# The order of high and low matrix products in a decoder trunk, and the rows that they read

## The chip, the core and the metric

The kernel runs on one core of a Trainium2 chip. The metric is the time of one execution on the device in microseconds; three runs of the kernel before were taken, and their median counts. Beside the runs there is a profile, which records one execution instruction by instruction.

A core has engines that work side by side: TensorE (PE) for matrix products, with a queue of weight loads that overlaps them (PEld), VectorE (DVE), ScalarE (ACT), GpSimd (POOL), and SyncE (SP), which here issues transfers. On-chip memory (SBUF) has 128 partitions; the products collect in banks of a second memory (PSUM) of 2048 bytes per partition each.

## What is computed

One step of a decoder trunk of one layer, for 256 prompt tokens and 8 x 4 sample tokens, 288 columns in all:

```python
def trunk_layer(x, hist_conv, hist_pool, pos0, ...):
    h = rmsnorm(x, norm1_g)
    proj = jnp.einsum("btd,de->bte", h, w_in) + b_in
    a, gate, z = proj[..., :D_CONV], proj[..., D_CONV:2 * D_CONV], proj[..., 2 * D_CONV:]
    u = a * jax.nn.sigmoid(gate)
    u_ext = jnp.concatenate([hist_conv.astype(u.dtype), u], axis=1)
    c = jax.nn.silu(layernorm(depthwise_causal_conv(u_ext, conv_w, conv_b), ln_g, ln_b))
    z_ext = jnp.concatenate([hist_pool.astype(z.dtype), z], axis=1)
    d = multiscale_pool(z_ext, pos0)
    p = jnp.einsum("btgc,gce->btge", d, pool_w).reshape(bsz, T, D_POOL) * pool_scale
    mix = jnp.concatenate([c, p], axis=-1)
    x = x + jnp.einsum("btm,md->btd", mix, w_out)
    h2 = rmsnorm(x, norm2_g)
    f = jnp.square(jax.nn.relu(jnp.einsum("btd,df->btf", h2, w_ff1)))
    x = x + jnp.einsum("btf,fd->btd", f, w_ff2)
    return x, u_ext[:, -(CONV_W - 1):], z_ext[:, -(POOL_MAX - 1):]
```

The model width is 2048, the hidden width of the MLP 8192, and all data are float32. After the layer comes one more RMSNorm.

## The kernel before

**Layout.** Channels lie on the partitions, the 288 tokens along the free dimension. A block is 128 channels: 2048 channels are 16 blocks. The weights come from memory in tiles of 1024 rows by 256 columns, two loads of 512 KB each, in an order that the host has laid out.

**High and low parts.** The products run in a rounded float32 format (`F32R`). To keep precision, every operand is split into a high part, its rounded value, and a low part, what the rounding left over. For the weights ScalarE casts a loaded tile `wr` into `whi` (line 257), and VectorE (262), GpSimd (265) or a transfer that adds (260) makes `wlo`. Each of these pools holds five tiles of four blocks of rows by 256 columns. The activations are split by ScalarE and VectorE in the same way, into tiles called `hx`, `dx`, `mx`, `ax` and `fx` by stage.

**The rows of an activation tile.** `act2` (line 117) makes a tile for two neighbouring channel blocks m = 0 and 1. It has four rows of 288 float32 numbers, 1152 bytes each, in the order low 0, high 0, low 1, high 1. So row 0 of a partition starts at byte 0, row 1 at 1152, row 2 at 2304, row 3 at 3456. Two of the `ax` pairs use a stretch of an older tile (`ax45`, line 565) in the same order, and the last two pairs use tiles of two rows each, low then high (line 570).

**The matrix routine.** `gemm` (line 283) takes a list of PSUM banks and a list `rhs` of channel blocks as (high, low) pairs. For every block k, and within it for every bank m, it issues three products with a weight tile of 128 x 128 as the stationary operand and a row of 288 columns as the moving operand: high weights x high row (297), high weights x low row (298), low weights x high row (299). The dropped fourth, low x low, is below the precision wanted. All of a bank's products add up in that bank. Usually there are two banks, one for each 128 columns of the weight tile; the first call has four.

**The stages**, in the order of time: the first call on `hx` for two channel blocks of the convolution at once, while the first weights arrive; then the rest of w_in on `hx`, with the depthwise convolution on VectorE and GpSimd (line 415), the gates and the pooling between; the four small pool products on `dx` (`pool_products`); w_out on `dx` and `mx`; then four rounds of eight calls with w_ff1 on `ax`, whose results become `fx`, and eight calls with w_ff2 on `fx`. A call with 16 blocks and two banks has 96 products, and there are 8112 products in all. The first call has 192, w_ff1 and w_ff2 have 3072 each.

**What sets the order.** The order of the engine queues is made when the kernel is built, by a scheduler with a simulated timeline: it takes the lines in program order and moves instructions forward that it believes ready. `between` and `issue_after` hold a few of them in place. In the first call the scheduler shuffles the products of the four banks; in the other calls they stay in program order. The ring of five tiles in each weight pool decides when ScalarE may cast the next tile: after the last product that reads the old one.

Of the kernel before, what the change touches and what calls it, by code (L numbers as in the profile page):

```python
# [10 lines left out]
F32R = mybir.dt.float32r  # L11
# [5 lines left out]
P = 128  # L17
# [3 lines left out]
T = SEQ + NB * NS  # L21
# [62 lines left out]
def trunk_kernel(ctx: ExitStack, tc: tile.TileContext, io):  # L84
# [3 lines left out]
    nc = tc.nc  # L88
# [5 lines left out]
    actp = ctx.enter_context(tc.tile_pool(name="actp", bufs=8))  # L94
# [8 lines left out]
    def nm(s):  # L103
        seen[s] = seen.get(s, 0) + 1
        return f"{s}{seen[s]}"
# [8 lines left out]
    def row(name):  # L114
        return rowp.tile([P, T], F32, name=nm(name), tag="row")

    def act2(name, **kw):

        t = actp.tile([P, 2, 2, T], F32R, name=nm(name), **(kw or {"tag": "act"}))
        return t[:, :, 1, :], t[:, :, 0, :]  # L120

    def tmp(name, n=T, tag="tmp", bufs=2):
        return tmpp.tile([P, n], F32, name=nm(name), tag=tag, bufs=bufs)
# [4 lines left out]
    def f32(t):  # L128
        return t.bitcast(F32)
# [15 lines left out]
    def v(key, j):  # L145
        return vec[:, OFF[key] + j : OFF[key] + j + 1]
# [136 lines left out]
    def gemm(banks, rhs, m_outer=False, between={}):  # L283


        n = len(rhs)
        gets = ready.pop()
        order = [(k, m) for k in range(n) for m in range(len(banks))]
        if m_outer:
            order.sort(key=lambda km: km[1])  # L290
        for k, m in order:
            if m == 0:
                ahead = between[k]() if k in between else None
            (xh, xl), b = rhs[k], banks[m][:, :T]
            wh, wl = gets[k // 8](k % 8, m)
            with tc.issue_after(ahead.ins) if ahead is not None else nullcontext():
                nc.tensor.matmul(b, wh, xh, start=k == 0, stop=False)  # L297
                nc.tensor.matmul(b, wh, xl, start=False, stop=False)  # L298
                last = nc.tensor.matmul(b, wl, xh, start=False, stop=k == n - 1)  # L299
        ready.extend(itertools.islice(weights, 1))  # L300
        return last.ins

    def bank2():
        return acc.tile([P, 2, 512], F32, name=nm("ac"), tag="ac")

    def each(bk):
        return [bk[:, m, :] for m in range(2)]

    def halves(x2):

        return [(x2[0][:, m, :], x2[1][:, m, :]) for m in range(2)]
# [4 lines left out]
    def first_split(k0, n):  # L316
        for k in range(k0, k0 + n):
            if k % 2 == 0:
                hx.extend(halves(act2("hx")))
            hh, hl = hx[k]  # L320
            nc.scalar.activation(hh, xT[:, k, :], AF.Copy, scale=v("norm1_g", k))
            nc.vector.scalar_tensor_tensor(out=hl, in0=xT[:, k, :], scalar=v("norm1_g", k), in1=f32(hh), op0=ALU.mult, op1=ALU.subtract)
        if k0 % 2 == 0:
            firsts.append([by_pair(t) for t in spl()])
        at = slice(k0 % 2, k0 % 2 + n)
        raw, hi, lo = (t[:, :, at, :] for t in (raws[k0 // 2], *firsts[k0 // 2]))
        split_part(raw, None, hi, lo, "V")
# [58 lines left out]
    def conv_products(i, **kw):  # L386
        history(i)
        banks = each(bank2())
        gemm(banks, hx, **kw)
        return banks  # L390
# [38 lines left out]
    def pool_group(g):  # L429
        nc.sync.dma_start(z_all[:, 2 * g : 2 * g + 2, ZO:ZL], io["hist_p"][:, 2 * g : 2 * g + 2, :])  # L430
        bk = bank2()
        gemm(each(bk), hx)
        z = z_all[:, 2 * g : 2 * g + 2, :]
        tz = tmpp.tile([P, 2, T], F32, name=nm("tz"), tag="ag", bufs=2)
        nc.vector.tensor_tensor(tz, bk[:, :, :T], both(rb), op=ALU.mult)
        for m in range(2):
            b_in = v("b_in", 16 + 2 * g + m)
            nc.scalar.activation(z[:, m, PH:ZO], tz[:, m, 0:SEQ], AF.Identity, bias=b_in)
            nc.scalar.activation(samples(z[:, m, ZO:ZL], ZS)[:, :, PH:ZS], samples(tz[:, m, SEQ:T], NS), AF.Identity, bias=b_in)
        s, w = z, 1  # L440
        while w < WINDOWS[g]:
            s2 = tmpp.tile([P, 2, ZL], F32, name=nm("s"), tag="s", bufs=2)
            for m in range(2):
                nc.gpsimd.tensor_tensor(s2[:, m, 2 * w - 1 :], s[:, m, 2 * w - 1 :], s[:, m, w - 1 : ZL - w], op=ALU.add)
            s, w = s2, 2 * w
        d = tmpp.tile([P, 2, T], F32, name=nm("d"), tag="ag2", bufs=2)
        first_sums = s[:, :, PH : PH + w - 1]
        nc.gpsimd.tensor_tensor(first_sums, first_sums, rcnt[:, None, w - 2 : 2 * w - 3].to_broadcast([P, 2, w - 1]), op=ALU.mult)
        nc.vector.scalar_tensor_tensor(out=d[:, :, 0:SEQ], in0=s[:, :, PH:ZO], scalar=1.0 / w, in1=z[:, :, PH:ZO], op0=ALU.mult, op1=ALU.subtract)  # L449
        news = [x[:, :, ZO:ZL].rearrange("p m (b t) -> p m b t", t=ZS)[:, :, :, PH:] for x in (s, z)]  # L450
        for m in range(2):
            nc.gpsimd.tensor_scalar(news[0][:, m], news[0][:, m], 1.0 / w, None, op0=ALU.mult)
            nc.gpsimd.tensor_tensor(samples(d[:, m, SEQ:T], NS), news[0][:, m], news[1][:, m], op=ALU.subtract)
        dh, dl = act2("dx", tag="p", bufs=4)
        nc.scalar.copy(dh, d)
        nc.vector.tensor_tensor(dl, d, f32(dh), op=ALU.subtract)  # L456
        dd[g] = dh, dl
# [3 lines left out]
    def pool_products(g):  # L461

        bk = ms("pp")
        gemm(each(bk), halves(dd[g]))
        for m, (mh, ml) in enumerate(halves(dd[g])):
            i = 2 * g + m
            nc.scalar.activation(mh, bk[:, m, :T], AF.Copy, scale=v("pool_scale", i))
            nc.vector.scalar_tensor_tensor(out=ml, in0=bk[:, m, :T], scalar=v("pool_scale", i), in1=f32(mh), op0=ALU.mult, op1=ALU.subtract)
            mixp[i] = (mh, ml)
# [62 lines left out]
    for g in range(8):  # L532
        bk = bank2()
        with behind:
            last = gemm(each(bk), [mixp[k] for k in korder], between=BETWEEN.get(g, {}))
# [5 lines left out]
    for j, c in enumerate(cs):  # L541
        n = tmpp.tile([P, 2, T], F32, name=nm("n"), tag="ag", bufs=2)
        nc.vector.tensor_tensor(n, c, norm["rows"][:, None, :].to_broadcast([P, 2, T]), op=ALU.mult)
        for m in range(2):
            i = 2 * j + m
            nc.scalar.activation(n[:, m, :], n[:, m, :], AF.Silu, bias=v("ln_b", i), scale=v("ln_g", i))
        mh, ml = act2("mx")
        nc.scalar.copy(mh, n)
        nc.vector.tensor_tensor(ml, n, f32(mh), op=ALU.subtract)
        mixc += halves((mh, ml))  # L550
# [4 lines left out]
    for g in range(8):  # L555
        bk = bank2()
        gemm(each(bk), mixc)
        x2 = xT[:, 2 * g : 2 * g + 2, :]
        nc.vector.tensor_tensor(x2, x2, bk[:, :, :T], op=ALU.add)
        if g < 4:  # L560
            a2 = halves(act2("ax", tag="p", bufs=4))
        elif g < 6:
            if g == 4:
                ax45 = zp.tile([P, N8 * ZL], F32R, name="ax45", tag="z")
                ax45 = ax45[:, 32 : 32 + 8 * T].rearrange("p (g m q t) -> p g m q t", g=2, m=2, q=2)
            a2 = halves((ax45[:, g - 4, :, 1, :], ax45[:, g - 4, :, 0, :]))
        else:
            a2 = []
            for m in range(2):
                t2 = actp.tile([P, 2, T], F32R, name=nm("ax"), tag="c", bufs=4)  # L570
                a2.append((t2[:, 1, :], t2[:, 0, :]))
        for m, (ah, al) in enumerate(a2):
            k = 2 * g + m
            xk = xT[:, k, :]
            nc.scalar.activation(ah, xk, AF.Copy, scale=v("norm2_g", k))
            nc.vector.scalar_tensor_tensor(out=al, in0=xk, scalar=v("norm2_g", k), in1=f32(ah), op0=ALU.mult, op1=ALU.subtract)
            x1.append((ah, al))
            if k == 0:
                nc.scalar.activation(ss2, xk, AF.Square)
            else:  # L580
                q2 = tmp("q")
                nc.scalar.activation(q2, xk, AF.Square)
                nc.gpsimd.tensor_tensor(ss2, ss2, q2, op=ALU.add)
# [4 lines left out]
    for ch in range(DFF // FCH):  # L588
        fx = []
        for g in range(FCH // 256):  # L590
# [4 lines left out]
            t = tmpp.tile([P, 2, T], F32, name=nm("t"), tag="ag", bufs=2)  # L595
# [7 lines left out]
        last = ch == DFF // FCH - 1  # L603
        for g in range(8):
            bk = bank2()
            banks = each(bk)
# [3 lines left out]
            for m in range(2):  # L610
                k = 2 * g + m
# [79 lines left out]
```

## Time and profile before

| | |
|---|---|
| runs, device time | 1106.66, 1105.6, 1106.64 us; median 1106.64 |
| profiled execution, first to last instruction | 1103.1 us |
| outside that span, against the three runs | 2.5 to 3.6 us |
| granted TensorE clock, mean over the span | 0.996 |
| memory traffic | 185.68 MB read, 4.28 MB written |

The profile's page has no time for its own execution apart from the span; the runs lie 2.5 to 3.6 us above that.

How to read the lines that follow. An instruction is named by its line in the kernel and by what it writes and reads, as in `ac<-ax,whi`: the bank `ac` from activations `ax` and high weights `whi`. `x1024` is a count. In the groups, the first number after the bar is the busy time in us and the second the mean of one in ns; then comes the idle time of the engine just before, with what ended it. Products are pipelined: one lasts longer in the records than the distance to the next, so that their rate is read from the starts. In the view by stretches each row has the window, its length, then busy time and count of PE, PEld, DVE, ACT and POOL, the granted clock, the busy share of the DMA engines and GB/s; where the view is for one engine, only that engine stands there.

### The profile page before, as it was taken

How to read it: one execution, taken by the hardware profiler on the slowest of the kernel's cores; microseconds unless marked ns; L12 is line 12 of the kernel's file. 1: busy time of each engine (PE TensorE's matmuls, PEld its weight loads, DVE VectorE, ACT ScalarE, POOL GpSimd, SP SyncE). 2: the span in 40 equal slices, each digit the busy share in tenths (PEclk: the TensorE clock that was granted, in tenths of full speed). 3: DMA queues.
4: the chain of work that ended last, by engine and by line, in shares of the span. 5: the costliest groups of instructions: out<-in, count | busy, mean ns of one | idle time of the engine just before them, and what ended most of it. 6: DMA issues, size and time to landing. Idle time of an engine off the chain costs nothing.

```text
span 1103.1 us, 19716 instructions
## 1 busy us (share of the span) xinstructions
PE 1087.3 (99%) x8204; PEld 1085.0 (98%) x8204; DVE 638.2 (58%) x814; ACT 477.8 (43%) x585; POOL 179.1 (16%) x209
## 2 busy tenths in 40 slices
PE   9999999999999999999999999999999999999996
PEld 8999999999999999999999999999999999999996
DVE  7889999787555444445544444545544445554553
ACT  8654445565544433333443333444433334444441
POOL 0879989512000000000000000000000000000000
PEclk9999999999999999999999999999999999999998
DMA  9996568555555555555555555555555555555522
GB/s 334 279 275 176 155 159 245 168 169 162 166 161 170 168 162 168 171 161 165 170 167 162 171 163 165 171 168 161 169 170 160 168 171 164 165 170 163 164 75 86
DMA packets 58265, 191.24 MB, mean 173 GB/s; under 512 B 6208, under 2 KB 11328, under 8 KB 58176
## 3 DMA queue, kind: packets, MB, share of 16 engines
q1 hardware_dynamic: 56752, 185.53, 53.7%
q0 software_dynamic: 1152, 4.19, 2.1%
q8 instruction: 64, 1.05, 0.4%
q10 hardware_dynamic: 272, 0.26, 0.1%
q14 instruction: 25, 0.20, 0.0%
HBM read 185.68 MB, written 4.28 MB: 172 GB/s over the span
## 4 chain that ended last, share of the span: by engine, by line
PE 89%; DVE 8%; DMA 1%; issue 1%; ACT 1%; POOL 0%; SPq 0%; DVEq 0%; POOLq 0%
PE ac L297 30%; PE ac L299 30%; PE ac L298 29%; DVE pc L415 3%; DVE wlo L262 1%; DMA wlo<-in_w 1%; DVE xT L631 0%; DMA wr<-in_w 0%; DVE c L421 0%; POOL prd L419 0%; DVE q L521 0%; DVE dx L456 0%; DVE c L515 0%; PE pt L242 0%; DVE d L449 0%
## 5 line engine op out<-in xcount | busy, mean ns | idle before, releaser
L257 ACT CAST whi<-wr 128x1024 fp32r<-128x1024 f32 (+1 forms) x341 | 355.6, 1043 | 570.8 <-PE ac L298 537.1
L262 DVE TENSOR_TENSOR wlo<-wr,whi 128x1024 fp32r<-128x1024 f32 (+1 forms) x295 | 363.1, 1231 | 353.4 <-ACT whi L257 352.3
L297 PE MATMUL ac<-ax,whi 128*128 128x288 f32 x1024 | 303.2, 296 | 0.0
L297 PE MATMUL ac<-fx,whi 128*128 128x288 f32 x1024 | 303.1, 296 | 0.0
L299 PE MATMUL ac<-ax,wlo 128*128 128x288 f32 x1024 | 301.9, 295 | 0.0
L299 PE MATMUL ac<-fx,wlo 128*128 128x288 f32 x1024 | 301.9, 295 | 0.0
L298 PE MATMUL ac<-ax,whi 128*128 128x288 f32 x1024 | 298.5, 292 | 0.0
L298 PE MATMUL ac<-fx,whi 128*128 128x288 f32 x1024 | 298.5, 292 | 0.0
L298 PEld LDWEIGHTS ac<-fx,whi 128*128 128x128 f32 x1024 | 192.5, 188 | 0.0
L298 PEld LDWEIGHTS ac<-ax,whi 128*128 128x128 f32 x1024 | 192.5, 188 | 0.0
L297 PEld LDWEIGHTS ac<-ax,whi 128*128 128x128 f32 x1024 | 192.4, 188 | 0.0
L297 PEld LDWEIGHTS ac<-fx,whi 128*128 128x128 f32 x1024 | 192.4, 188 | 0.0
L299 PEld LDWEIGHTS ac<-ax,wlo 128*128 128x128 f32 x1024 | 191.5, 187 | 0.0
L299 PEld LDWEIGHTS ac<-fx,wlo 128*128 128x128 f32 x1024 | 191.5, 187 | 0.0
L297 PE MATMUL ac<-hx,whi 128*128 128x288 f32 x384 | 113.4, 298 | 1.3 <-ACT whi L257 1.3
L299 PE MATMUL ac<-hx,wlo 128*128 128x288 f32 x384 | 110.9, 295 | 1.0 <-DMA wlo<-in_w 0.8
L298 PE MATMUL ac<-hx,whi 128*128 128x288 f32 x384 | 111.4, 292 | 0.0
L265 POOL TENSOR_TENSOR wlo<-wr,whi 128x512 fp32r<-128x512 f32 x76 | 103.8, 1413 | 37.0 <-ACT whi L257 35.5
L415 DVE SCALAR_TENSOR_TENSOR pc<-u_all,vec,pc 128x256 f32<-128x256 f32 x232 | 99.7, 481 | 3.5 <-ACT pc L412 2.3
L297 PEld LDWEIGHTS ac<-hx,whi 128*128 128x128 f32 x384 | 72.3, 189 | 1.7 <-ACT whi L257 1.7
L299 PEld LDWEIGHTS ac<-hx,wlo 128*128 128x128 f32 x384 | 71.2, 188 | 1.5 <-DMA wlo<-in_w 1.0
L298 PEld LDWEIGHTS ac<-hx,whi 128*128 128x128 f32 x384 | 72.2, 188 | 0.0
(117 smaller groups left out, 826.8 us busy)
## 6 DMA issues: line engine op xcount, KB each, us to landing
wr<-in_w SPq DMA_DIRECT2D x335, 512.0 KB, 3.8
wlo<-in_w POOLq DMA_DIRECT2D x8, 512.0 KB, 7.3
xT<-in_xT SPq DMA_DIRECT2D x7, 288.0 KB, 8.0
wr<-in_w SPq DMA_DIRECT2D x5, 256.0 KB, 3.7
out_u_out<-u_all SPq DMA_DIRECT2D x1, 1208.0 KB, 8.6
out_yT<-xT SPq DMA_DIRECT2D x2, 576.0 KB, 2.9
u_all<-in_hist_c SPq DMA_DIRECT2D x8, 136.0 KB, 5.4
out_z_out<-z_all SPq DMA_DIRECT2D x1, 668.0 KB, 9.1
```

Of the source, the lines that this page charges most:

```text
L257: nc.scalar.copy(hi, raw)
L262: nc.vector.tensor_tensor(lo, raw, f32(hi), op=ALU.subtract)
L265: nc.gpsimd.tensor_tensor(lo[:, j : j + 2, :], raw[:, j : j + 2, :], f32(hi[:, j : j + 2, :]), op=ALU.subtract)
L297: nc.tensor.matmul(b, wh, xh, start=k == 0, stop=False)
L298: nc.tensor.matmul(b, wh, xl, start=False, stop=False)
L299: last = nc.tensor.matmul(b, wl, xh, start=False, stop=k == n - 1)
L415: nc.vector.scalar_tensor_tensor(out=dst, in0=up[:, w : w + SEQ], scalar=cwv[:, w : w + 1], in1=pc, op0=ALU.mult, op1=ALU.add)
```

## The change

A call of `gemm` with two banks now takes the blocks in pairs. For a pair and a bank it issues six products: high x high for the first block and the second, low weights x high row for the first and the second, then high weights x low row for the second and the first. So the high rows are read four times in a row and the low rows twice. The call with four banks keeps one block at a time and its order of three.

The rows of an activation tile are now low 0, high 0, high 1, low 1. The six products read rows 1, 2, 1, 2, 3, 0, which start at bytes 1152, 2304, 1152, 2304, 3456 and 0. The tiles with two rows (the last two `ax` pairs) hold low, high for m = 0 and high, low for m = 1. Nothing else changes: the number of products, their operands and the sums are the same. The products of a call add up in another order.

```diff
+    def rows(t):
+
+        return t[:, 1:3, :], t[:, 0:4:3, :]
+
     def act2(name, **kw):
 
-        t = actp.tile([P, 2, 2, T], F32R, name=nm(name), **(kw or {"tag": "act"}))
-        return t[:, :, 1, :], t[:, :, 0, :]
+        return rows(actp.tile([P, 4, T], F32R, name=nm(name), **(kw or {"tag": "act"})))
...
-        order = [(k, m) for k in range(n) for m in range(len(banks))]
+        step = 2 if len(banks) == 2 else 1
+        order = [(k, m) for k in range(0, n, step) for m in range(len(banks))]
         if m_outer:
             order.sort(key=lambda km: km[1])
-        for k, m in order:
+        for k0, m in order:
             if m == 0:
-                ahead = between[k]() if k in between else None
-            (xh, xl), b = rhs[k], banks[m][:, :T]
-            wh, wl = gets[k // 8](k % 8, m)
+                ahead = between[k0]() if k0 in between else None
+            b, todo = banks[m][:, :T], []
+            for k in range(k0, k0 + step):
+                (xh, xl), (wh, wl) = rhs[k], gets[k // 8](k % 8, m)
+                todo.append([(wh, xh), (wl, xh), (wh, xl)] if step == 2 else [(wh, xh), (wh, xl), (wl, xh)])
+            if step == 2:
+                (hh0, lh0, hl0), (hh1, lh1, hl1) = todo
+                todo = [[hh0, hh1, lh0, lh1, hl1, hl0]]
+            todo = sum(todo, [])
             with tc.issue_after(ahead.ins) if ahead is not None else nullcontext():
-                nc.tensor.matmul(b, wh, xh, start=k == 0, stop=False)
-                nc.tensor.matmul(b, wh, xl, start=False, stop=False)
-                last = nc.tensor.matmul(b, wl, xh, start=False, stop=k == n - 1)
+                for j, (w, x) in enumerate(todo):
+                    last = nc.tensor.matmul(b, w, x, start=k0 + j == 0, stop=k0 + step == n and j == len(todo) - 1)
...
-                ax45 = ax45[:, 32 : 32 + 8 * T].rearrange("p (g m q t) -> p g m q t", g=2, m=2, q=2)
-            a2 = halves((ax45[:, g - 4, :, 1, :], ax45[:, g - 4, :, 0, :]))
+                ax45 = ax45[:, 32 : 32 + 8 * T].rearrange("p (g r t) -> p g r t", g=2, r=4)
+            a2 = halves(rows(ax45[:, g - 4]))
...
-                a2.append((t2[:, 1, :], t2[:, 0, :]))
+                a2.append((t2[:, 1 - m, :], t2[:, m, :]))
```

## The prediction

> **What bounds the kernel now.** I read the page's busy shares first, then the chain of work that ended last, then the stretches of the span, and last the starts of single products.
>
> ```profile
> span 1103.1 us, 19716 instructions
> PE 1087.3 (99%) x8204; PEld 1085.0 (98%) x8204; DVE 638.2 (58%) x814; ACT 477.8 (43%) x585; POOL 179.1 (16%) x209
> ...
> PE 89%; DVE 8%; DMA 1%; issue 1%; ACT 1%; POOL 0%; SPq 0%; DVEq 0%; POOLq 0%
> PE ac L297 30%; PE ac L299 30%; PE ac L298 29%; DVE pc L415 3%; DVE wlo L262 1%; DMA wlo<-in_w 1%; DVE xT L631 0%; DMA wr<-in_w 0%; DVE c L421 0%; POOL prd L419 0%; DVE q L521 0%; DVE dx L456 0%; DVE c L515 0%; PE pt L242 0%; DVE d L449 0%
> ```
>
> TensorE sets the end: the three product lines of the one matrix routine are 89% of the chain. The next question is whether it waits inside the stages. The view by stretches answers it (busy time, instructions in brackets, granted clock, share and rate of the DMA engines):
>
> ```profile
> 5.00:33.00 28.00, 26.48 (x195) 25.83 (x194) 24.27 (x37) 22.68 (x39) 4.11 (x4) 1.00 1.02 371
> 33.00:165.00 132.00, 131.21 (x993) 130.97 (x993) 124.07 (x260) 69.44 (x97) 115.51 (x122) 1.00 0.74 203
> 165.00:216.00 51.00, 48.91 (x364) 47.69 (x363) 43.93 (x82) 25.47 (x33) 43.44 (x37) 1.00 0.69 211
> 216.00:290.00 74.00, 74.00 (x565) 74.00 (x564) 56.25 (x58) 43.70 (x68) 14.30 (x15) 1.00 0.53 167
> 290.00:1089.00 799.00, 799.00 (x6049) 799.00 (x6047) 382.53 (x370) 312.78 (x344) 0.00 (x0) 1.00 0.51 160
> 1089.00:1103.00 14.00, 3.75 (x34) 3.56 (x33) 6.45 (x12) 1.18 (x3) 0.00 (x0) 0.72 0.43 169
> ...
> 400.00:1000.00 600.00, 600.00 (x4539) 1.00 0.53 166
> ```
>
> From 216 to 1089 us TensorE has no idle time in the records, at full granted clock, while VectorE, ScalarE and the DMA engines are about half busy. Only the spacing of the products counts there. In the last row 600 us hold 4539 products: 132.2 ns from start to start. Before 216 us VectorE is the near rival: 124.1 of 132 us.
>
> Is 132.2 ns fixed by the size, or by the operands? The groups by line say that equal sizes do not cost the same:
>
> ```profile
> L297 PE MATMUL ac<-ax,whi 128*128 128x288 f32 x1024 | 303.2, 296 | 0.0
> L299 PE MATMUL ac<-ax,wlo 128*128 128x288 f32 x1024 | 301.9, 295 | 0.0
> L298 PE MATMUL ac<-ax,whi 128*128 128x288 f32 x1024 | 298.5, 292 | 0.0
> ```
>
> The durations overlap and their ends are modelled, so I take only the differences from them; starts carry the sum. In the timeline of the steady stage the order is L297 (high x high), L298 (high x low), L299 (low x high):
>
> ```profile
> 700.12 0.29 PE L298 MATMUL ac<-ax,whi 128*128 128x288 f32 x1
> ...
> 700.91 0.29 PE L298 MATMUL ac<-ax,whi 128*128 128x288 f32 x1
> ```
>
> Six products lie between these two starts: 0.79 us, 131.7 ns each within the 10 ns of the view, in agreement with 132.2.
>
> **The change part by part.** Counts first. The number and size of products, weight loads, splits, evictions and DMAs stay as they are. What is new is which moving operand follows which, and which weights.
>
> *The step between moving operands.* One row of a tile is 288 x 4 = 1152 bytes. Before, a triple reads rows high, low, high, and the next triple begins on the same row or two rows on: steps of -1152, +1152, then 0 or 2304. After, six products of a pair read rows 1, 2, 1, 2, 3, 0, and the next six begin at row 1 again: steps of +1152, -1152, +1152, +1152, -3456, +1152. 1152 and 3456 are odd multiples of 128 bytes, 0 and 2304 even ones. In the built programs every third step was even; after, none in the last two stages, 8 of 1775 in the stages from the third channel block to w_out.
>
> The trace of before has a place where odd steps alone follow each other: the first product routine, with four banks, which the scheduler shuffled so that L297 and L298 alternate (rows 1, 0, 1, 0):
>
> ```profile
> 23.73 0.30 PE L297 MATMUL ac<-hx,whi 128*128 128x288 f32 x1
> 23.87 0.29 PE L298 MATMUL ac<-hx,whi 128*128 128x288 f32 x1
> 23.99 0.29 PE L297 MATMUL ac<-hx,whi 128*128 128x288 f32 x1
> 24.13 0.29 PE L298 MATMUL ac<-hx,whi 128*128 128x288 f32 x1
> 24.25 0.29 PE L297 MATMUL ac<-hx,whi 128*128 128x288 f32 x1
> 24.39 0.29 PE L298 MATMUL ac<-hx,whi 128*128 128x288 f32 x1
> 24.51 0.29 PE L299 MATMUL ac<-hx,wlo 128*128 128x288 f32 x1
> ...
> 24.91 0.56 PE L299 MATMUL ac<-hx,wlo 128*128 128x288 f32 x3
> 25.31 0.29 PE L297 MATMUL ac<-hx,whi 128*128 128x288 f32 x1
> ...
> 26.89 0.30 PE L297 MATMUL ac<-hx,whi 128*128 128x288 f32 x1
> ...
> 27.67 0.30 PE L299 MATMUL ac<-hx,wlo 128*128 128x288 f32 x1
> ...
> 30.05 0.30 PE L297 MATMUL ac<-hx,whi 128*128 128x288 f32 x1
> ...
> 30.57 0.29 PE L299 MATMUL ac<-hx,wlo 128*128 128x288 f32 x1
> ```
>
> From 23.73 to 24.51 six spacings take 0.78 us, from 26.89 to 27.67 again 0.78, from 30.05 to 30.57 four take 0.52: 130 ns each, three times. The opposite stands between: three L299 in a row, all even steps, take 0.40 us, 133.3 ns each. So I take 130.0 ns for the new order against 132.2: an estimate of 2.2 ns saved per product. The stretches are short, half of their steps keep the weights, and none has a step of 3456, so both ends stay open: from above 133.3, below.
>
> *From below.* The shortest spacing is what every step might become. The view of line L298 gives shortest and median:
>
> ```profile
> L298 PE MATMUL ac<-ax,whi x1024: 288/295/297, 275.3 to 986.9; 128*128 128x288 f32 x171
> ```
>
> 288 against the mean of the three lines, (296 + 295 + 292) / 3 = 294.3, is 6.3 ns less; it stands for a floor of 132.2 - 6.3 = 125.9 ns.
>
> *The sum.* From 216 to 1089 us stand 565 + 6049 = 6614 instructions, 6600 of them these products: 6600 x 2.2 ns = 14.5 us. From 33 to 216 us stand 993 + 364 = 1357: 3.0 us at most. There TensorE was already waiting 2.9 us, and VectorE would be 124.1 busy of 130; I count half, 1.5. In the first routine the order of one block at a time stays, and it is bound by 371 GB/s of loads: nothing. The tail after 1089 us is VectorE's and a DMA's: nothing. Together 16.0 us, span 1103.1 to 1087.1.
>
> The three runs are 1105.6 to 1106.66, median 1106.64, so 2.5 to 3.6 us lie around the span; with 3.5 the forecast is 1090.6.
>
> *Buffers.* The last product of a pair now reads the high weights of the first block (low x high came last before), so a `whi` tile is free one product later, 0.13 us, and a `wlo` tile two earlier. What waits for the former is ScalarE's cast of new weights:
>
> ```profile
> ACT whi L257 <- PE ac L298: 537.1, 291, 3.4
> DVE wlo L262 <- ACT whi L257: 352.3, 259, 3.5
> ...
> L262 DVE TENSOR_TENSOR wlo<-wr,whi 128x1024 fp32r<-128x1024 f32 x189 | 231.7, 1226 | 265.8 <-ACT whi L257 265.8
> L257 ACT CAST whi<-wr 128x1024 fp32r<-128x1024 f32 x190 | 199.8, 1052 | 372.2 <-PE ac L298 372.2
> ```
>
> ScalarE stands idle for it 1.85 us on average; cast and subtraction take 2.3 us together, and the ring has five tiles, each 24 products or 3.2 us of work, so a tile is needed again some 12 us after it is freed. Cover 10 us against 0.13: nothing. If it were gone, each of some 290 tiles would pay 0.13 us, 38 us in all. Behind ScalarE's cast queue the activations' splits; VectorE's subtraction waits for the cast.
>
> *Operands needed earlier.* The second block of a pair is now read at the second product instead of the seventh, 5 x 0.13 = 0.66 us earlier. Only the last pair of a stage is fresh, and it is read 84 products or 11 us after the stage's first: covered. In the four pool products (one pair each, 12 products) both blocks are fresh, but one cast writes them together, so nothing; the first w_out products may lose 0.66 us once. The scheduler also swaps some of VectorE's, ScalarE's and GpSimd's work before 216 us, and one weight load with the `u_out` store on SP; that is in the half I left out.
>
> **The rivals.**
> *Spacing set by load and product together, no matter the addresses.* For it: the weight loads are as busy as the products, 1085.0 of 1103.1 us, and 130 rests on 16 spacings read to 10 ns. Against it: three stretches agree, and even steps give 133.3. It gives 132.2 ns, 1106.6 us.
> The Trainium skill says the same from another side: "TensorE: Matmul & The Clock Gate", section "Back-to-back issue gap", makes the gap the column count over 2.4 GHz plus 2.5 ns, 122.5 ns for 288 columns, with no address in it. The rows above, 132.2 and uneven, do not follow that figure; its consequence for the order would be this rival's, 1106.6 us.
>
> *New weights for each product cost more than repeated ones.* Before, L298 uses the weights of L297 again, and has the shortest duration, 292; after, no two neighbours share weights. The price is that of the L299 run, whose weights all differ: 133.3 - 132.2 = 1.1 ns on 7957 products, 8.8 us: 1115.4, slower. It decides as soon as the new order costs over 132.5 ns (2.2 us, 0.2% of the time, over 7957). Against it: in the alternating stretch the change to new weights (23.87 to 23.99, 0.12 us) is followed by less spacing than the repeat (23.99 to 24.13, 0.14).
>
> *All steps at the floor.* 125.9 ns: 6600 x 6.3 = 41.6 us, and before 216 us half of 8.5, as VectorE becomes the bound there: 1106.6 - 45.9 = 1060.7. For it: after, five of six steps are of one kind (+1152 or -3456), in the stretch only half; the +1152 steps there show 0.12, 0.12 and 0.12 us (0.14 for -1152).
>
> **How the numbers follow.** Chances: forecast 0.55 (own range 1083 to 1098, by 129.0 and 131.0 ns), floor 0.17, no effect 0.14, weights 0.14. Over 0.2%, 2.2 us, is what a measurement here tells from nothing. Faster 0.72, same 0.12, slower 0.16, since each case frays a little. The range runs from 1058, which holds the floor, to 1110, which takes in no effect and the mildest loss; only the weights rival is left out.
>
> **What would show it.** Right: the steady stage at 129 to 131 ns (600 us holding 4580 to 4650 instead of 4539), no idle of TensorE after 216 us, the casts of `whi` still waiting for TensorE. The no-effect rival: 4539 again. The weights rival: fewer than 4530. The floor: over 4750. The early stages decide 1.5 us: TensorE's idle there should grow from 2.9 to about 4.4. The forecast is wrong if even steps were not what cost 133.3.

## The result, and the profile after

| | before | after |
|---|---|---|
| median of six runs each | 1106.12 us (1104.96 to 1108.46) | 1116.57 us (1115.39 to 1117.85) |
| ratio, 95% interval | | 1.0087 [1.0073, 1.0102] |
| span of the profiled execution | 1103.1 us | 1115.1 us |

The change costs 0.9%, clear of the noise, where 1.4% less was forecast: outside the range and on the other side. The page of the changed kernel, its first lines and its chain of work:

```profile
span 1115.1 us, 19604 instructions
PE 1097.2 (98%) x8204; PEld 1095.2 (98%) x8204; DVE 639.4 (57%) x814; ACT 478.9 (43%) x585; POOL 178.6 (16%) x209
...
PE ac L308 92%; DMA wlo<-in_w 1%; DMA wr<-in_w 1%; POOL wlo L268 1%; ACT whi L260 1%; ACT hx L330 1%; PE pp L308 0%; DMA xT<-in_xT 0%; DVE xT L640 0%; ACT z_all L379 0%; POOL prd L428 0%; DVE sum_c L516 0%; PE idle L228 0%; PE pt L245 0%; PE pt L225 0%
```

Line 308 is the one product line of the changed routine. TensorE still sets the end, with the same 8204 instructions. In the view by stretches (columns as before: PE, PEld, DVE, ACT, POOL, clock, DMA share, GB/s) two things have changed:

```profile
33.00:165.00 132.00, 130.63 (x979) 130.16 (x979) 123.41 (x256) 69.41 (x98) 114.89 (x120) 1.00 0.72 205
165.00:216.00 51.00, 47.64 (x343) 46.84 (x342) 44.60 (x82) 24.17 (x32) 44.99 (x39) 0.97 0.67 202
216.00:290.00 74.00, 74.00 (x558) 74.00 (x557) 56.91 (x59) 42.77 (x68) 14.24 (x15) 1.00 0.50 164
290.00:1089.00 799.00, 799.00 (x5998) 799.00 (x5997) 382.99 (x367) 314.32 (x342) 0.00 (x0) 1.00 0.50 161
400.00:1000.00 600.00, 600.00 (x4503) 600.00 (x4502) 282.72 (x258) 227.66 (x235) 0.00 (x0) 1.00 0.51 165
```

First, TensorE is as busy as before and at full clock, but 600 us hold 4503 products instead of 4539. Products overlap the edges of a window, some three of them in this count, so the spacing is 600 / 4500 = 133.3 ns, where before it was 600 / 4536 = 132.3. Read from start to start over the whole w_ff2 stage the two are 133.33 and 132.22 ns. On the 6139 spacings of the last two stages that is 6.8 us, and some 1.1 ns on 1750 products ahead of them 1.9 us.

Second, the stretch from 165 to 216 us has less busy time (47.64 against 48.91 us) and a lower clock (0.97 against 1.00). The view of what TensorE waits for names one wait: that of the layer norm's mean for VectorE's sum. After, then before (us in total, times, longest):

```profile
PE pmean L519 <- DVE sum_c L517: 3.3, 1, 3.3
```

```profile
PE pmean L510 <- DVE sum_c L508: 1.3, 1, 1.3
```

Most of the longer wait lies in the addition just before that sum. It took 2.63 us, where the same addition took 1.14 us before; why it took longer was not tried. After, then before:

```profile
199.04 2.63 DVE L516 TENSOR_TENSOR sum_c<-sum_c,c 128x576 f32<-128x576 f32 x1
```

```profile
197.43 1.14 DVE L507 TENSOR_TENSOR sum_c<-sum_c,c 128x576 f32<-128x576 f32 x1
```

The timeline of the changed kernel shows what follows on it:

```profile
199.47 0.43 PE L308 MATMUL ac<-dx,whi 128*128 128x288 f32 x2
203.16 0.75 PE L519 MATMUL pmean<-sum_c,ones 128*128 128x288 f32 x2 [3.26 <-DVE sum_c L517]
...
204.46 1.16 PE L308 MATMUL ac<-dx,whi 128*128 128x288 f32 x4
205.42 0.68 PE L308 MATMUL ac<-dx,wlo 128*128 128x288 f32 x2
205.90 1.16 PE L308 MATMUL ac<-dx,whi 128*128 128x288 f32 x4
```

The four products at 204.46 and the two at 205.42 take 0.96 and 0.48 us from start to start, 240 ns each: behind the wait of 3.26 us some 14 products run at half speed, 1.5 us lost on top of 2.0 us more wait. The Trainium skill, page "TensorE: Matmul & The Clock Gate", section "HAM oscillation — how this bites in real kernels", says that an idle time beyond about 3.4 us halves the clock; the trace agrees in kind, with 3.26 us of idle by the records, slightly under that figure, and a granted clock of 0.97 in the stretch.

In the other runs too a wait for the mean of 3.2 us or more has a half clock behind it (`m4`, 3.2 us, clock 0.97 in the stretch; `n4`, 5.1 us, 0.93), and one of 3.1 us has none (`n1`, clock 1.00). The length of one wait is not the whole rule: in the first call `r1` has the half clock from 12.1 to 15.5 us, where its longest wait was 1.8 us.

The parts are 6.8 + 1.9 + 2.0 + 1.5 = 12.2 us, and the spans differ by 12.0. By the starts, the first w_ff1 product comes at 280.3 us instead of 275.2, so that 5.1 us of the loss lie ahead of it. The rest of the study asks why the spacing rose.

### The profile page after: what moved, and what is told of

Read it like the earlier page. It is cut to its first block, busy times and chain, and to the rows that moved or that the text cites. A ratio compares the mean times of both kernels' runs of the same rounds, so it can differ in the third digit from the quotient of the medians.

```text
span 1115.1 us, 19604 instructions
## 1 busy us (share of the span) xinstructions
PE 1097.2 (98%) x8204; PEld 1095.2 (98%) x8204; DVE 639.4 (57%) x814; ACT 478.9 (43%) x585; POOL 178.6 (16%) x209
## 3 DMA queue, kind: packets, MB, share of 16 engines
q0 software_dynamic: 1152, 4.19, 2.1%
## 4 chain that ended last, share of the span: by engine, by line
PE 93%; DMA 2%; ACT 2%; DVE 1%; POOL 1%; issue 1%; SPq 0%; DVEq 0%; POOLq 0%
PE ac L308 92%; DMA wlo<-in_w 1%; DMA wr<-in_w 1%; POOL wlo L268 1%; ACT whi L260 1%; ACT hx L330 1%; PE pp L308 0%; DMA xT<-in_xT 0%; DVE xT L640 0%; ACT z_all L379 0%; POOL prd L428 0%; DVE sum_c L516 0%; PE idle L228 0%; PE pt L245 0%; PE pt L225 0%
## 5 line engine op out<-in xcount | busy, mean ns | idle before, releaser
L308 PE MATMUL ac<-ax,whi 128*128 128x288 f32 x2048 | 357.7, 296 | 0.0
L308 PE MATMUL ac<-fx,whi 128*128 128x288 f32 x2048 | 357.3, 296 | 0.0
L308 PEld LDWEIGHTS ac<-fx,whi 128*128 128x128 f32 x2048 | 301.5, 189 | 0.0
L308 PEld LDWEIGHTS ac<-ax,whi 128*128 128x128 f32 x2048 | 301.5, 189 | 0.0
L308 PE MATMUL ac<-fx,wlo 128*128 128x288 f32 x1024 | 220.1, 296 | 0.0
L308 PE MATMUL ac<-ax,wlo 128*128 128x288 f32 x1024 | 220.1, 296 | 0.0
L308 PE MATMUL ac<-hx,whi 128*128 128x288 f32 x768 | 136.9, 297 | 1.5 <-ACT whi L260 1.5
L308 PE MATMUL ac<-dx,whi 128*128 128x288 f32 x256 | 46.8, 302 | 0.0
L308 PE MATMUL ac<-mx,whi 128*128 128x288 f32 x256 | 44.7, 296 | 0.0
L308 PEld LDWEIGHTS ac<-dx,whi 128*128 128x128 f32 x256 | 39.1, 194 | 0.1
```

Of the source, the lines that this page charges most:

```text
L308: last = nc.tensor.matmul(b, w, x, start=k0 + j == 0, stop=k0 + step == n and j == len(todo) - 1)
```

## The experiments

Steps are distances between the starts of successive moving operands. A spacing in this part is the mean from start to start of a run's products in the w_ff2 stage, unless it names another. The one row quoted for a kernel is the stretch from 600 to 1000 us: TensorE's busy time, count, clock, DMA share and GB/s. As it reads for the kernel before and for the changed one:

```profile
600.00:1000.00 400.00, 400.00 (x3027) 1.00 0.53 166
```

```profile
600.00:1000.00 400.00, 400.00 (x3003) 1.00 0.51 165
```

So 3027 stands for 132.2 ns, 3003 for 133.3, and 3040 for 131.7. The kernels of `m`, `n1` to `n3`, `p` and `s1` were run once each; they are read for their spacing, and not for small differences of time. In the code cuts, `...` marks lines left out.

### One half of the change at a time

`r1_old_order`: the new rows with the old order of products.

```diff
-        step = 2 if len(banks) == 2 else 1
+        step = 1
...
```

> The changed kernel with the order of before (high x high, high x low, low x high, one block and one bank at a time) on the new rows low, high, high, low. Two theories. Weights: a product that keeps the stationary operand of the one before it is cheaper, and the order of before has one such product in three, the new order none. Steps: the step between the starts of the moving operands decides, and odd multiples of 128 bytes, which the new order has everywhere, are dear. Weights theory: the steady stage is back at 132.2 ns per product, time 1105 to 1109 us. Steps theory: here five steps of six are odd (before four of six, after six of six), so the spacing stays nearer to after's, 132.7 to 133.3 ns, 1110 to 1116 us.

```profile
600.00:1000.00 400.00, 400.00 (x3040) 1.00 0.52 167
```

131.7 ns and 1102.21 us, ratio 0.9955 [0.9938, 0.9972] to before: faster than either theory said, and faster than the kernel before. The new rows alone are a gain. Only the last call of the stage is different: from 1073.74 to 1086.27 us, 94 spacings, it ran at 133.3 ns. That call issues all products of one bank before those of the other, so that its rows run 1, 0, 1, 2, 3, 2 and all its steps are odd; the table below comes back to it.

`r2_old_rows`: the new order on the old rows.

```diff
-        return t[:, 1:3, :], t[:, 0:4:3, :]
+        return t[:, 1:4:2, :], t[:, 0:3:2, :]
...
-                a2.append((t2[:, 1 - m, :], t2[:, m, :]))
+                a2.append((t2[:, 1, :], t2[:, 0, :]))
```

> The changed kernel with the new order of products on the old rows low, high, low, high. Two steps of six are odd multiples of 1152 bytes, four are 2304, and no product keeps the weights of the one before it. Weights theory: 133.3 ns per product in the steady stage as after, 1114 to 1118 us. Steps theory: with fewer odd steps than before, at or under 132.2 ns, 1107 us or less.

```profile
60.00:160.00 100.00, 100.00 (x746) 1.00 0.64 185
600.00:1000.00 400.00, 400.00 (x3028) 1.00 0.51 166
...
165.00:216.00 51.00, 47.54 (x344) 0.97 0.68 201
```

132.2 ns in the late stages, where no product repeats weights: the weights theory misses. The steps theory misses the time, which it put at 1107 us or less. The first row tells why: 134.4 ns in the w_in stage (758 products there before), with the same order and rows; and from 165 to 216 us the clock is 0.97 and the busy time 47.54 us, as in the changed kernel. Together 1110.63 us, 1.0036 [1.0024, 1.0048]. Neither half of the change has the spacing of both.

### Two other orders in the pair

`r3_two_repeats` and `r4_shifted`: the new rows, with the six products in another order.

```diff
-                todo = [[hh0, hh1, lh0, lh1, hl1, hl0]]
+                todo = [[hh0, hl0, hh1, hl1, lh0, lh1]]
```

> The changed kernel with another order in each pair: high x high and high x low of the first block, the same of the second, then the two low x high products. Weights repeat at the second and the fourth of six products, so the two repeats lie two products apart; before they lay three apart, and there the saving showed at every second repeat only (six products in 793.3 ns where after takes 800.0). Weights theory, if each repeat saves 3.3 ns: 132.2 ns, 1105 to 1109 us. Weights theory, if a repeat saves 6.7 ns but only at one parity of the product's number: 131.1 ns, 1096 to 1100 us, or 133.3 ns, 1114 to 1118 us, by the parity. Steps theory: four odd steps of six as before, 132.2 ns.

131.7 ns, 1101.52 us, ratio 0.9950 [0.9931, 0.9969]: the lowest median of all, within the noise of `r1`. In six calls of the w_in stage it ran at 134.4 ns like the run before it, then at 131.7 in the same stage with the same pattern.

```diff
-                todo = [[hh0, hh1, lh0, lh1, hl1, hl0]]
+                todo = [[lh0, hh0, hl0, hh1, hl1, lh1]]
```

> As the run before it, but one product later: low x high of the first block, high x high and high x low of the first, the same of the second, low x high of the second. Repeats at the third and the fifth of six products. Weights theory, each repeat 3.3 ns: 132.2 ns, 1105 to 1109 us. Weights theory with parity: the opposite of the run before if the parity is tied to the start of a call (131.1 against 133.3 ns); the same as the run before if only the distance between repeats counts. Steps theory: four odd steps of six, 132.2 ns.

131.7 ns, 1104.26 us, 0.9980 [0.9968, 0.9993]. No parity shows. The number of 131.7 had not been offered by any theory with a repeat worth 3.3 or 6.7 ns. But in the w_in stage, from 60.4 to 166.2 us, this kernel too ran at another value, 133.3 ns:

```profile
61.00:161.00 100.00, 100.00 (x752) 1.00 0.65 186
```

The changed kernel also has 752 products in 100 us of that stage, `r1` 761.

### What the spacing is made of

Three kernels leave work out, and one moves the tiles. `m1_cols256` and `m2_weights64` narrow all products but the first of a bank (and the last, in the second kernel). In these edits and the like ones below, the product then writes `o` in place of `b`.

```diff
+                    o = b
+                    if step == 2 and k0 + j > 0:
+                        o, x = b[:, :SEQ], x[:, :SEQ]
```

> The changed kernel with products of 256 columns instead of 288 (all but the first of each bank), so the sample tokens' results are left out of all later products. If the moving operand sets the spacing (288 columns plus a fixed part), it falls by 32 columns, that is by about 13 ns to 120 ns, and the span to about 1010 us. If the weight load or the issue of the two instructions sets it, 133.3 ns stay and the span stays at 1115 us.

```profile
600.00:1000.00 400.00, 400.00 (x3368) 1.00 0.55 177
```

118.9 ns, span 1020.9 us: 32 columns fewer take off 14.5 ns. The number of columns, moved and written, sets most of the spacing.

```diff
+                    o = b
+                    if step == 2 and k0 + j > 0 and not (k0 + step == n and j == len(todo) - 1):
+                        o, w = b[:64, :], w[:, :64]
```

> The changed kernel with weights of 64 columns instead of 128 in all products but the first and the last of each bank, so half of the output channels are left out. If the weight load sets the spacing, it falls from 133.3 ns to what the moving operand needs, 120 to 126 ns. If the moving operand or the issue of instructions sets it, 133.3 ns stay.

```profile
600.00:1000.00 400.00, 400.00 (x3040) 1.00 0.52 167
```

131.7 ns, with weight loads of 136 ns in place of 188. The edit takes off 1.7 ns, not the 7 to 13 expected of a load that bounds, and not nothing: the load is not the bound. It also halves the rows that a product writes, so whether the 1.7 ns come from the load is not shown.

```diff
+                    o = b
+                    if step == 2:
+                        x = rhs[k0][0]
```

> The changed kernel with the same moving row, the high row of the first block, in all six products of a pair: steps of 0 within a bank and a pair, and the weights in the new order; the products with the low rows and the second block are left out. Row theory (the steps between moving operands set the spacing, odd multiples of 1152 bytes everywhere give 133.3 ns): a spacing below 133.3 ns, 132.2 or less. If the steps do not matter and the new order of the weights does: 133.3 ns.

```profile
600.00:1000.00 400.00, 400.00 (x3002) 1.00 0.51 165
```

133.3 ns: odd steps are not what is dear; steps of 0 give the same.

`m4_pad128` puts 128 bytes between the weight tiles and the activation tiles.

```diff
+    padp = ctx.enter_context(tc.tile_pool(name="padp", bufs=1))
+    gap = padp.tile([P, 32], F32, name="gap")
+    nc.gpsimd.memset(gap, 0.0)
     actp = ctx.enter_context(tc.tile_pool(name="actp", bufs=8))
```

> The changed kernel with all activation tiles moved by 128 bytes against the weight tiles; every step and every order is as before that. Row theory: 133.3 ns in the steady stage as without the move, span 1115 us. Meeting theory (the weight load and the moving operand are read side by side, and where the two addresses meet sets the spacing): another spacing than 133.3 ns.

133.3 ns, span 1114.1 us: a move of 128 bytes against the weights changes nothing. That speaks against the meeting of two addresses; other distances were not tried.

### Weights or steps

After these runs two theories stood: repeats of weights, or steps that are all of one kind. `n1_one_row_old` and `n2_alternate_old` take the old order of weights, so that one product in three repeats them, with uniform steps; `n3_one_weight` takes one weight block for all.

```diff
-        step = 2 if len(banks) == 2 else 1
+        step = 1
...
+                    o = b
+                    if len(banks) == 2:
+                        x = rhs[k0 - k0 % 2][0]
```

> The new rows with the order of weights of before (high, high, low: one weight block in three is used twice in a row), and one moving row, the high row of the first block, for all twelve products of a pair: all steps even (0 or multiples of 4608). The products with the low rows and the second block are left out. Uniform theory: when all steps between moving operands are of one kind (all even or all odd multiples of 128 bytes), the spacing is 133.3 ns whatever the weights, as in the run with one row and the new order. Weights theory: the repeats save 1.1 to 2.2 ns per product, 131.1 to 132.2 ns.

133.3 ns. `n2` differs from it in one line:

```diff
-                        x = rhs[k0 - k0 % 2][0]
+                        x = rhs[k0 - k0 % 2][(3 * (k0 if m_outer else m) + j) % 2]
```

> As the run before it, but the moving operand alternates between the high and the low row of the first block, so that all steps are odd (1152, -1152 or -3456) while the weights repeat as before: the stretch on which the forecast rested, made the rule everywhere. The second block's products are left out. Forecast: 130.0 ns. Uniform theory: 133.3 ns. Weights theory: 131.1 to 132.2 ns.

```profile
600.00:1000.00 400.00, 400.00 (x3003) 1.00 0.51 165
```

133.3 ns. These are the alternating rows of the forecast's own stretch, run everywhere: they have the changed kernel's spacing. (The weights repeat at one product in three here, at every second one in the stretch.) Yet 130.0 ns comes up in this run as well, once: from 168.82 to 172.72 us, in w_out, 30 spacings take 3.90 us.

```profile
168.82 0.29 PE L311 MATMUL ac<-dx,wlo 128*128 128x288 f32 x1
...
172.72 0.29 PE L311 MATMUL ac<-dx,wlo 128*128 128x288 f32 x1
```

Pool products follow it, and behind them the same rows run at 133.3 ns.

```diff
+                    o = b
+                    if step == 2:
+                        w = gets[k0 // 8](k0 % 8, 0)[0]
```

> The changed kernel with its rows and order of moving operands, but one weight block, the high weights of the first block, for all twelve products of a pair; the products with the other weights are left out. Uniform theory: 133.3 ns, since all steps are still odd. Weights theory: with eleven repeats of twelve, 130 ns or less.

133.3 ns, with eleven repeats in twelve. Repeated weights save nothing in these three runs, whose steps are all of one kind; whether they matter where steps are mixed was not separated.

`n4_mirror`, meant as a faster version, mixes the steps again:

```diff
-                todo = [[hh0, hh1, lh0, lh1, hl1, hl0]]
+                todo = [[hh0, hl0, lh0, lh1, hh1, hl1]]
```

> The changed kernel's rows with the order high x high, high x low, low x high of the first block, then low x high, high x high, high x low of the second: rows 1, 0, 1, 2, 2, 3, four odd steps and two even ones, and two repeats of weights. It is meant to be a faster version. Uniform theory: as the other mixed orders, 131.7 or 132.2 ns, 1100 to 1107 us. Weights theory: as the other orders with two repeats of six, 131.7 or 132.2 ns.

131.7 ns as expected of a mixed order, but 1106.63 us, 1.0004 [0.9991, 1.0017]. The wait for the mean is 5.1 us here, 3.8 more than before, and with the clock behind it takes up the gain:

```profile
165.00:216.00 51.00, 45.27 (x324) 0.93 0.64 195
```

```profile
PE pmean L519 <- DVE sum_c L517: 5.1, 1, 5.1
```

### Which kind of step

`p1_rows1280` is the kernel before with rows 1280 bytes apart, `p2_rows1216` the same with 1216 (304 columns).

```diff
-    wraw = ctx.enter_context(tc.tile_pool(name="wraw", bufs=6))
+    wraw = ctx.enter_context(tc.tile_pool(name="wraw", bufs=4))
...
-        t = actp.tile([P, 2, 2, T], F32R, name=nm(name), **(kw or {"tag": "act"}))
-        return t[:, :, 1, :], t[:, :, 0, :]
+        t = actp.tile([P, 2, 2, 320], F32R, name=nm(name), **(kw or {"tag": "act"}))
+        return t[:, :, 1, :T], t[:, :, 0, :T]
...
```

> The kernel before, with its order and its sequence of rows, but rows 1280 bytes apart instead of 1152 (32 columns of padding; two raw weight tiles fewer make the room). All steps are now multiples of 256 bytes: 0, 1280, 2560. If what counts is whether a step is an odd or an even multiple of 128 bytes, all steps are of one kind and the steady spacing goes from 132.2 to 133.3 ns. If what counts is whether the next product reads the same row, the neighbour or the one after it, 132.2 ns stay.

```profile
600.00:1000.00 400.00, 400.00 (x3040) 1.00 0.52 167
```

131.7 ns; one run took 1103.3 us. All steps are even multiples of 128 bytes, and still it is not 133.3, so that the parity is not the kind. Nor did the 132.2 of before stay.

> As the run before it, with rows 1216 bytes apart (19 times 64): steps of 1216 are odd multiples of 64 bytes, 2432 is an odd multiple of 128, 0 an even one. Steps of several kinds are mixed, so if the kind of a step counts at all, the spacing is not 133.3 ns; 131.7 or 132.2 ns by the other mixed orders. If the neighbourhood of rows counts, 132.2 ns.

132.8 ns in most calls, 131.7 in four of the w_out stage, and 133.3 in the last call, which again goes bank by bank: for the rest another value, not 133.3.

What fits the w_ff2 stage of all runs with 288 columns, full weights and rows 1152 or 1280 bytes apart is the step modulo 512 bytes, in three classes: 0, 128 on either side, and 256. With 1280 the steps are of the classes 0 and 256. (In `p2` the 1216 bytes are 192 off a multiple of 512, in none of the three.) That was found after the fact, so one more run tried the class 256 alone, which none had had. `s1_far_rows` starts from `r2_old_rows`:

```diff
+                    o = b
+                    if step == 2:
+                        x = rhs[k0 + j % 2][0]
```

> The new order of weights on the old rows, with the moving operand alternating between the high row of the first and of the second block, 2304 bytes apart: every step, from tile to tile too, is 256 bytes beyond a multiple of 512. The low rows' products and some of the high ones are left out. Class theory: a step falls into one of three classes by its distance from a multiple of 512 bytes (0, 128 on either side, 256); with one class alone the spacing is 133.3 ns, with two or three mixed it is not. Here one class, 256, which no run had alone: 133.3 ns in the steady stage. If only the classes 0 and 128 have that, because their runs had the same row or neighbours throughout: another value, 131.7 to 132.8 ns.

```profile
600.00:1000.00 400.00, 400.00 (x3002) 1.00 0.51 165
```

133.3 ns, as the classes said in advance.

The table collects the kernels with 288 columns and 128 weights; classes are counts in twelve products of the w_ff2 stage.

| kernel | class 0 | class 128 | class 256 | products in 400 us | spacing, ns |
|---|---|---|---|---|---|
| after, `m4`, `n2`, `n3`, `q1` | 0 | 12 | 0 | 3002 or 3003 | 133.3 |
| `m3`, `n1` | 12 | 0 | 0 | 3002, 3003 | 133.3 |
| `s1` | 0 | 0 | 12 | 3002 | 133.3 |
| before | 2 | 8 | 2 | 3027 | 132.2 |
| `r2` | 0 | 4 | 8 | 3028 | 132.2 |
| `r1` | 2 | 10 | 0 | 3040 | 131.7 |
| `r3` | 0 | 8 | 4 | 3040 | 131.7 |
| `r4`, `n4` | 2 | 8 | 2 | 3041, 3040 | 131.7 |
| `p1` | 4 | 0 | 8 | 3040 | 131.7 |

The last call of `r1` is the same comparison inside one run: twelve of class 128 there, and 133.3 ns, where the calls ahead of it are mixed and have 131.7. The other way round the rule fails: `r4` reads the same mixed rows in w_in as in w_ff2, and had 133.3 ns there. So every kernel of the table with a single class had 133.3 ns in w_ff2, and a mixture had mostly, not always, another value.

### How much is the early part

`q1_late_pairs` keeps the new rows and takes the pairs only for w_ff1 and w_ff2.

```diff
-    def gemm(banks, rhs, m_outer=False, between={}):
+    def gemm(banks, rhs, m_outer=False, between={}, pairs=False):
...
-        step = 2 if len(banks) == 2 else 1
+        step = 2 if pairs else 1
...
-            gemm(each(bk), x1)
+            gemm(each(bk), x1, pairs=True)
...
-            gemm(banks, fx, m_outer=last and g == 7)
+            gemm(banks, fx, m_outer=last and g == 7, pairs=True)
```

> The changed kernel's rows, its order of pairs only in the w_ff1 and w_ff2 stages, and the order of before in all stages ahead of them. If the loss of the change is the spacing in the steady stage plus a loss of its own in the early stages (the longer wait for the layer norm's mean, and the lower clock behind it), this one has the first part alone: 133.3 ns there, 131.7 ns ahead, and the sum over the run with the old order everywhere is 6139 x 1.65 ns = 10.1 us, about 1112 us, without a wait of 3.9 us near 200 us. If the whole loss is the spacing, it comes within 1 us of the changed kernel, 1116 us.

```profile
165.00:216.00 51.00, 48.75 (x364) 1.00 0.67 213
```

```profile
PE pmean L519 <- DVE sum_c L517: 1.3, 1, 1.3
```

1111.89 us, 1.0055 [1.0038, 1.0072], with 133.3 ns in the late stages, 131.7 in w_in, a wait of 1.3 us and full clock. (The wait of 3.9 us in the expectation is 3.3 us in the changed kernel's view.) Against `r1_old_order`, 1102.21, the late pairs cost 9.7 us (10.1 expected); against the changed kernel, 1116.57, the early stages hold the other 4.7.

## Why the prediction was wrong, point by point

*What bounds the kernel: right.* TensorE's spacing sets the end, and 32 columns fewer (`m1`) moved the span by 94 us.

*Spacing depends on the operands, not on the size alone: right.* Orders and rows alone moved it between 131.7 and 134.4 ns. The Trainium skill's 122.5 ns ("TensorE: Matmul & The Clock Gate", "Back-to-back issue gap") is the spacing of no run with 288 columns, and its consequence, no effect of the order, did not hold; the section gives that formula for a single product and says that in a stream with weight loads both set the spacing.

*The step that failed: "So I take 130.0 ns for the new order against 132.2".* The prediction read three stretches of four and six spacings as the rate of alternating rows. Made the rule (`n2`), alternating rows have 133.3 ns. The 130.0 ns were no misreading: `n2` itself has them over 30 spacings. But they did not last, and a short stretch did not stand for the rate of thousands of products; why it settled there is open. The sign of the effect was wrong too: in the classes modulo 512 bytes the change takes a mixed sequence (2, 8, 2) to a single class (0, 12, 0), and single classes had 133.3 ns in all eight kernels of the table that have them. The step that was taken for the dear one, an even multiple of 128 bytes, belongs to the mixture with which the kernel before ran at 132.2. So 6600 x 2.2 ns of gain became 6139 x 1.1 ns of loss in the two big stages.

*The bounds of that step.* That "both ends stay open: from above 133.3" came from the run of three L299, and the outcome is just that number, in part by luck, since the prediction took it for the price of even steps; the range, though, left out the rival that used it. The middle and this end were read in the same way, from 16 spacings and from three, so that 0.55 against 0.14 was more trust than such stretches bear.

*The floor: not reached.* No kernel with 288 columns ran its w_ff2 stage below 131.7 ns.

*The weights rival: right in its number, wrong in its reason.* It gave 1115.4 us and fewer than 4530 products, and 1116.57 us and 4503 came. But `r2` repeats no weights and has 132.2 ns in the late stages, `n1` and `n2` repeat them as before and have 133.3, and `n3` hardly ever changes them and has 133.3. The price came out right by luck, as far as the weights go: its source, the three L299 in a row, has steps of one kind, as the changed kernel has. Without experiments the time would have been taken for a proof of the mechanism.

*The early stages: wrong by sign and size.* "I count half, 1.5" of a gain; some 5 us of loss came: 5.4 as a sum (1.9 by spacing, 2.0 by the wait for the mean, 1.5 by the clock), 5.1 by the starts. The prediction named the scheduler's swaps ahead of 216 us and did not price them. VectorE's sum ended later there, by 1.5 us in one addition; which of the moved instructions delayed it was not tried. `q1` shows only that with the old order in the early stages the wait is 1.3 us again.

*Buffers and operands needed earlier: nothing, as said.* No wait for weights or rows appears after 300 us, and ScalarE's casts still wait for TensorE.

## What to carry to other kernels

Where TensorE has no gaps, its spacing can still move by 1 to 2% with where each moving operand starts against the last, and with the stage in which a sequence runs. Read it from a count over hundreds of products that repeat one pattern, and never from a handful inside another pattern. An order of products that is made regular on purpose should be tried beside an irregular one with the same work: here an irregular one (`r3`) is 0.5% faster than before, the regular one 0.9% slower. A change of order in one routine also reorders the scheduler's other engines, and in these runs a wait for the mean of 3.2 us or more was paid twice, by the clock behind it.

## What was not expected of the hardware

The spacing is not a sum of prices, one for each step. It settles at a few values, which repeat to some hundredths of a ns over whole calls: 131.67, 132.22, 133.33 and 134.44 ns, that is 790, 793.3, 800 and 806.7 ns for six products. Neighbours differ by 3.3 or 6.7 ns in six. Within a value the single spacings are uneven: near 700 us the changed kernel repeats 131, 131, 131 and 140 ns over four products, the kernel before 126, 131, 134, 132, 133 and 137 over six, each to within 1 ns.

The same order and rows can settle at two of them: `r2` runs at 134.4 ns in the w_in stage and at 132.2 after it, `r3` at 134.4 and 131.7, `r4` at 133.3 and 131.7. In `r3` the value changed at 114.5 us without any idle time, where one pool product came between those of w_in; and behind six small `pt` products, near 216 us, it was at 134.4 again until 231. In `r2` it changed near 165 us, where w_out begins. Why a sequence settles where it does stays open. The classes tell single ones (133.3 in w_ff2) from mixed ones there, not which value a mixed sequence takes: before, `r4` and `n4` have the same counts, and 132.2, 131.7 and 131.7 ns in w_ff2. And they are not the whole: `m2`, with class 128 alone, half the weight columns and half the rows written, had 131.7 ns, in a way that these runs do not resolve.
